# First layer's inputs by quarters of the features

## The chip, the cores and the metric

One core of one Trainium2 chip runs the kernel. The metric is the device time of one execution in microseconds, lower is better. Three runs of the kernel before took 2805.35, 2808.10 and 2808.39 us; the median is 2808.1.

## The reference, cut to what matters

The model is two blocks one after the other over 512 tokens of 1024 features, all float32: a first block of two layers with modulation and several mixers, then a second block with its own mixers and feed-forward layers. The change touches the very beginning, the first layer's normalised and modulated inputs and the first projection made of them. A second stream, ctx, has 256 tokens and runs through the first layer too.

```
m = silu(cvec) @ w_ada + b_ada             # w_ada is 1024 x 3072; cvec is c for x, c_ctx for ctx
sh, sc, gt = split(m, 3)
h  = rms(x,   norm_w) * (1 + sc)   + sh    # 512 x 1024
hc = rms(ctx, norm_w) * (1 + sc_c) + sh_c  # 256 x 1024
p  = h @ w_in                              # k and v columns of two attentions first: 2 x 256 of 2816
```

sh and sc are needed before any product of h: for feature f, sh[f] and sc[f] are columns f and 1024 + f of the modulation.

## The kernel before, in words

A product in full precision is three matmuls: each operand is split into a rounded high part and a low rest, and high x high, high x low and low x high are added in PSUM (`mm3`, L237). The split of a weight or an input takes a cast on ScalarE and a subtraction on VectorE or GpSimd (`wload` L219, `split` L256).

`layer0_norm` (L429) squares and scales the tokens of one stream and transposes them, feature tile by feature tile (eight tiles of 128 features), so that the features lie on the partitions. `ada0` (L451) makes the modulation columns of one half of the features, for both streams: it loads 512 columns of sh and 512 of sc for each of the eight 128-row blocks of `w_ada`, multiplies them by silu(c) and silu(c_ctx), copies the result, transposes it and adds the bias. The four 32-column groups of TensorE's array take the two row blocks of a pair and sh and sc, so two groups are added up at the end.

`proj_kv0` (L499) is the stage of the change. `inputs(i, h)` modulates and splits four feature tiles of stream i; `products(i, h)` adds their products with the 512 k and v columns into six PSUM banks, one for each of four x and two ctx tiles of 128 tokens. One feature tile is 12 matmuls for x and 6 for ctx. `weights(h)` loads and splits the 512 rows of `w_in` that belong to a half. The code runs ada half 0, weights 0, inputs of x, then products of x while ada half 1 is loaded and multiplied between them; then ctx with half 0, weights 1, and both streams with half 1.

Buffers order the rest. Weights and the first half's first four modulation row blocks share the tag `wraw` (two buffers of 8 KB a partition); the other modulation loads have the tag `ada` (four buffers of 4 KB). A load whose buffer is taken waits until its last reader is through. PSUM transposes and the later modulation products share two banks (`tp`).

No engine runs its instructions in the order of the program. A planner in the compiler goes through the program with modelled times and gives each engine, at each moment, the earliest instruction of the program whose inputs and buffers it takes to be ready. The order is then fixed, and each engine runs its list in order, SyncE its DMA issues too.

Of the kernel before, what the change touches and what calls it, by code (L numbers as in the profile page):

```python
# [9 lines left out]
F32 = mybir.dt.float32  # L10
# [4 lines left out]
ALU = mybir.AluOpType  # L15
AX = mybir.AxisListType
PSUM = bass.MemoryType.PSUM
P = 128
# [78 lines left out]
class Kern:  # L97
# [331 lines left out]
    def layer0_norm(self, i, hcp):  # L429

        xt, nt = self.toks[i]
        ss = self.tl(self.sm, [P, nt], F32, "l0ss")
        sq = self.tl(self.hp, [P, 1024], BF16, "hhi")
        for t in range(nt):
            self.S.activation(sq, xt[:, t, :], AF.Square, accum_out=ss[:, t:t + 1])
        r = self.rsq(ss, 1.0 / 1024, EPS, [P, nt], "nrm")
        for t in range(nt):
            self.V.tensor_scalar(xt[:, t, :], xt[:, t, :], r[:, t:t + 1], None, ALU.mult)
        n = nt * P
        xn = [self.tl(*((self.xp, [P, 512], F32, "x"), (hcp, [P, 256], F32, "xc"))[i]) for _ in range(8)]  # L440
        yield xn, n
        for k in range(8):
            ps = self.tl(self.tp, [P, 512], F32, "tp")
            for t in range(nt):
                self.T.transpose(ps[:, t * P:(t + 1) * P], xt[:, t, k * P:(k + 1) * P], self.ident)
            (self.S.copy if k % 2 else self.V.tensor_copy)(xn[k], ps[:, :n])
            if k == 3:
                yield
        yield

    def ada0(self, h, pool):  # L451

        w = self.I["w_ada"][0][:, 0:2048].rearrange("p (a h n) -> p a h n", a=2, h=2)[:, :, h, :]
        bad, nw = self.col("b_ada", 0), self.col("norm_w", 0)
        ad = self.ad[0]

        def load(k):
            raw = self.tl(pool, [P, 2, 512], F32, "ada", bufs=4)
            self.nc.sync.dma_start(raw, w[k * P:(k + 1) * P])
            return raw  # L460

        raws = []
        if h == 0:
            for k in (0, 2):
                raw = self.tl(self.wp, [P, 2, 2, 512], F32, "wraw")
                for r in range(2):
                    self.nc.sync.dma_start(raw[:, r], w[(k + r) * P:(k + r + 1) * P])
                    raws.append(raw[:, r])
        n0 = len(raws)
        raws += [load(k) for k in range(n0, n0 + 4)]  # L470
        yield

        ps = self.mt() if h == 0 else self.tl(self.tp, [P, 512], F32, "tp")
        for k2 in range(4):
            for r in range(2):
                raw = raws.pop(0)
                for a in range(2):
                    g = 2 * r + a
                    self.T.matmul(ps[32 * g:32 * g + 32, :], self.sT[:, 2 * k2 + r, :], raw[:, a, :], start=(k2 == 0), stop=(k2 == 3))
            if n0 == 0 and k2 < 2:  # L480
                raws += [load(k) for k in (2 * k2 + 4, 2 * k2 + 5)]
            if k2 < 3:
                yield
        sb = self.tl(pool, [P, 2, 512], F32, "ada", bufs=4)[:, 0]
        self.V.tensor_copy(sb, ps)
# [3 lines left out]
        ptv = pt.rearrange("p (b r) -> p b r", b=4)  # L489
        for g in range(4):  # L490
            for i in range(2):
                o = 8 * (g % 2) + 4 * h
                dst = ad[:, i, o:o + 4]
                self.V.tensor_tensor(dst, ptv[:, :, 32 * g + i], bad[:, o:o + 4] if g < 2 else dst, ALU.add)
        o = 4 * h
        for i in range(2):
            self.V.scalar_tensor_tensor(ad[:, i, 8 + o:12 + o], ad[:, i, 8 + o:12 + o], 1.0, nw[:, o:o + 4], ALU.add, ALU.mult)

    def proj_kv0(self, ada, st, hcp):  # L499


        ap = self.pool(st, "qkv")
        kvt = [self.tl(ap, [P, 6, 256], F32, "hkv", bufs=2) for _ in range(2)]
        acts, res = [[], []], []
        norms = [self.layer0_norm(i, hcp) for i in range(2)]

        def inputs(i, h):
# [8 lines left out]
        def products(i, h):  # L516
            for k in range(4):
                for tt in ((0, 1, 2, 3), (4, 5))[i]:
                    hi, lo = (t[:, tt % 4 * P:(tt % 4 + 1) * P] for t in acts[i][4 * h + k])
                    self.mm3(pss[tt], hi, lo, w[0][:, k, :], w[1][:, k, :], h + k == 0, h == 1 and k == 3)  # L520
                yield

        def weights(h):
            return self.wload([self.I["w_in"][0][512 * h:512 * h + 512, c0:c0 + 256].rearrange("(k p) n -> p k n", p=P)
                               for c0 in (256, 1024)], 4, 512)

        res.append(next(norms[0]))
        next(norms[0])
        for _ in ada:
            pass  # L530
        w = weights(0)
        self.toks.append(self.load_tok(self.l0p, 1))
        inputs(0, 0)
        pss = [self.mt() for _ in range(6)]
        ada = self.ada0(1, self.l0p)
        next(ada)
        pr = products(0, 0)
        next(pr)
        next(norms[0])
        next(pr)  # L540
        next(ada)
        res.append(next(norms[1]))
        next(norms[1])
        inputs(1, 0)
        next(ada)
        for _ in pr:
            pass
        next(norms[1])
        for _ in ada:
            pass  # L550
        for _ in products(1, 0):
            pass
        w = weights(1)
        inputs(0, 1)
        inputs(1, 1)
        for _ in itertools.chain(products(0, 1), products(1, 1)):
            pass
# [597 lines left out]
    def every(self, gen, n):  # L1155

        for _ in gen:
            for _ in range(n):
                yield
# [1215 lines left out]
```

## Time and profile before

| | us |
|---|---|
| median of three runs | 2808.1 |
| profiled execution | 2807.09 |
| its span (first to last instruction) | 2805.3 |
| TensorE busy in the span | 2712.3 |
| first product of the projection starts | 34.24 |
| its last product ends, about | 80.3 |

The span is what the profiler saw of one execution; durations are read from it. A timeline row gives start, duration, engine, line, operation, output<-inputs, shape and count; in brackets the engine's idle time before it and what ended it. "SPq" is a DMA issue of SyncE, "PE" a matmul of TensorE ("MATMUL" is also a transpose), DVE is VectorE, ACT ScalarE, POOL GpSimd. Rows with a count above 1 cover several instructions in a row.

### The profile page before, as it was taken

Reading aid. Unit: us, or ns where it says so; the run is one execution under the profiler, and the core shown is the slowest. Engines: PE = TensorE matmul, PEld = TensorE weight load, DVE = VectorE, ACT = ScalarE, POOL = GpSimd, SP = SyncE. Lnnn points to the kernel's source line nnn. Section 1 sums busy time; section 2 is a strip of 40 time slices with the busy share of each in tenths; the row PEclk is TensorE's granted clock in tenths of the full one; section 3 lists DMA queues with packets and bytes.
Section 4 is the critical chain, followed back from the end, with each engine's and each line's share of the span. In section 5 each row is a group of like instructions: output and inputs, shape, how many; then the busy total and the mean of one; then the engine's idle time right before and its main releaser. Section 6 shows DMA issues by size and latency. Waiting matters only on the chain. (4 is left out here: it accounts for less than half of the span.)

```text
span 2805.3 us, 39529 instructions
## 1 busy us (share of the span) xinstructions
PE 2712.3 (97%) x15800; PEld 2259.3 (81%) x15800; DVE 1426.3 (51%) x2790; ACT 1001.8 (36%) x1804; POOL 916.7 (33%) x701
## 2 busy tenths in 40 slices
PE   7999999999998999999999989999999989999998
PEld 4976888888897888888988766788888866788888
DVE  5635511113255556434677787655542377655532
ACT  3335522222343553333445342422222344422322
POOL 4500343333234133333322235633333221333332
PEclk9999999999999999999999999999999999999999
DMA  7226222212222114342322230233233212332322
GB/s 248 68 85 201 64 64 69 63 57 68 91 78 90 46 49 122 119 134 76 95 84 71 52 100 31 76 92 104 90 98 98 79 54 84 101 102 91 97 95 87
DMA packets 221580, 250.32 MB, mean 89 GB/s; under 512 B 14351, under 2 KB 205428, under 8 KB 220116
## 3 DMA queue, kind: packets, MB, share of 16 engines
q1 hardware_dynamic: 219204, 242.86, 27.8%
q0 software_dynamic: 2192, 4.93, 0.9%
q8 instruction: 124, 2.03, 0.3%
q14 instruction: 60, 0.49, 0.1%
HBM read 233.64 MB, written 8.88 MB: 86 GB/s over the span
## 5 line engine op out<-in xcount | busy, mean ns | idle before, releaser
L234 POOL TENSOR_TENSOR wlo<-wraw,whi 128x1024 fp32r<-128x1024 f32 (+3 forms) x180 | 437.6, 2431 | 830.6 <-ACT whi L233 809.0
L233 ACT CAST whi<-wraw 128x1024 fp32r<-128x1024 f32 (+2 forms) x360 | 352.1, 1007 | 587.1 <-issue 197.9
L234 DVE TENSOR_TENSOR wlo<-wraw,whi 128x1024 fp32r<-128x1024 f32 (+2 forms) x180 | 235.6, 1309 | 376.0 <-ACT whi L233 375.5
L240 PE MATMUL ex<-hhi,wlo 128*128 128x512 f32 x1044 | 408.5, 391 | 6.8 <-DVE wlo L234 6.8
L238 PE MATMUL ex<-hhi,whi 128*128 128x512 f32 x1044 | 410.6, 393 | 0.6 <-ACT whi L233 0.6
L239 PE MATMUL ex<-hlo,whi 128*128 128x512 f32 x1044 | 408.4, 391 | 0.0
L238 PE MATMUL mm<-hhi,whi 128*128 128x512 f32 x708 | 281.8, 398 | 2.5 <-ACT whi L233 2.5
L239 PE MATMUL mm<-hlo,whi 128*128 128x512 f32 x708 | 279.1, 394 | 3.0 <-DVE hlo L330 2.6
L240 PE MATMUL mm<-hhi,wlo 128*128 128x512 f32 x708 | 279.2, 394 | 2.6 <-DVE wlo L234 2.5
L240 PEld LDWEIGHTS ex<-hhi,wlo 128*128 128x128 f32 x1044 | 196.9, 189 | 49.6 <-DVE wlo L234 8.4
L238 PEld LDWEIGHTS ex<-hhi,whi 128*128 128x128 f32 x1044 | 197.1, 189 | 41.7 <-ACT whi L233 1.2
L239 PEld LDWEIGHTS ex<-hlo,whi 128*128 128x128 f32 x1044 | 197.2, 189 | 39.7 <-issue 0.2
L238 PEld LDWEIGHTS mm<-hhi,whi 128*128 128x128 f32 x708 | 133.8, 189 | 32.8 <-issue 3.8
L240 PEld LDWEIGHTS mm<-hhi,wlo 128*128 128x128 f32 x708 | 133.7, 189 | 32.0 <-DVE wlo L234 3.6
L239 PEld LDWEIGHTS mm<-hlo,whi 128*128 128x128 f32 x708 | 133.7, 189 | 31.3 <-DVE hlo L330 3.9
L238 PE MATMUL mm<-whi,hhi 128*128 128x256 f32 (+1 forms) x464 | 135.5, 292 | 2.1 <-ACT hhi L258 2.1
L240 PE MATMUL mm<-whi,hlo 128*128 128x256 f32 (+1 forms) x464 | 133.3, 288 | 1.4 <-DVE hlo L330 1.4
L239 PE MATMUL mm<-wlo,hhi 128*128 128x256 f32 (+1 forms) x464 | 133.1, 287 | 0.6 <-DVE wlo L234 0.6
L238 PE MATMUL ex<-fhi,whi 128*128 128x512 f32 (+1 forms) x308 | 112.1, 364 | 0.0
L240 PE MATMUL ex<-fhi,wlo 128*128 128x512 f32 (+1 forms) x308 | 111.8, 363 | 0.0
L239 PE MATMUL ex<-flo,whi 128*128 128x512 f32 (+1 forms) x308 | 111.7, 363 | 0.0
L234 POOL TENSOR_TENSOR wblo<-wbraw,wbhi 128x256 fp32r<-128x256 f32 x32 | 27.0, 844 | 238.9 <-ACT wbhi L233 229.0
(827 smaller groups left out, 6024.4 us busy)
## 6 DMA issues: line engine op xcount, KB each, us to landing
wraw<-in_w_merge SPq DMA_DIRECT2D x32, 1024.0 KB
wraw<-in_ev_w_in SPq DMA_DIRECT2D x22, 1024.0 KB
wraw<-in_ffn_gate SPq DMA_DIRECT2D x22, 1024.0 KB
wraw<-in_ffn_up SPq DMA_DIRECT2D x22, 1024.0 KB
wraw<-in_w_in SPq DMA_DIRECT2D x20, 1024.0 KB
wraw<-in_ffn_down SPq DMA_DIRECT2D x17, 1024.0 KB
wraw<-in_w_ada SPq DMA_DIRECT2D x16, 1024.0 KB
wbraw<-in_w_br SPq DMA_DIRECT2D x32, 256.0 KB
```

The costliest lines, as they stand in the source:

```text
L233: self.S.copy(hi[:, a:b], raw[:, a:b])
L234: e.tensor_tensor(lo[:, a:b], raw[:, a:b], hi[:, a:b].bitcast(F32), ALU.subtract)
L238: self.T.matmul(ps, lh, rh, start=first, stop=False)
L239: self.T.matmul(ps, lh, rl, start=False, stop=False)
L240: self.T.matmul(ps, ll, rh, start=False, stop=last)
```

## The change

Quarters take the place of halves. `ada0(q)` makes the columns of 256 features of sh and of sc: eight loads of 128 x (2 x 256), four column groups for four row blocks, four partial sums that a reduction adds. The first quarter's eight row blocks lie in the two `wraw` buffers, the later quarters' in the four `ada` buffers, two row blocks in each. `layer0_norm` yields after every second feature tile. `inputs` and `products` do two feature tiles at a time; the matmuls of the products stay the same, 96 for x and 48 for ctx in all. ctx's first quarter is multiplied after the third quarter of x, its last three after the last of x. The copy of the modulation sums has a buffer of its own.

```diff
-            if k == 3:
+            if k % 2 and k < 7:
                 yield
...
+        w = self.I["w_ada"][0][:, 0:2048].rearrange("p (a h n) -> p a h n", a=2, h=4)[:, :, q, :]
+        for k in range(0, 8, 4 if q == 0 else 2):
+            if q == 0:
+                raw = self.tl(self.wp, [P, 4, 2, 256], F32, "wraw")
+            else:
+                raw = self.tl(pool, [P, 2, 2, 256], F32, "ada", bufs=4)
+            for r in range(raw.shape[1]):
+                self.nc.sync.dma_start(raw[:, r], w[(k + r) * P:(k + r + 1) * P])
+                raws.append(raw[:, r])
+        yield
+        ps = self.mt() if q == 0 else self.tl(self.tp, [P, 512], F32, "tp")
+        for k in range(8):
+            g = k % 4
+            self.T.matmul(ps[32 * g:32 * g + 32, :], self.sT[:, k, :], raws[k].rearrange("p a n -> p (a n)"), start=(k < 4),
+                          stop=(k >= 4))
             if k == 3:
                 yield
...
+        sb = self.tl(pool, [P, 512], F32, "adasb")
+        V.tensor_copy(sb, ps)
         pt = self.tl(self.tp, [P, 512], F32, "tp")
         for b in range(4):
             self.T.transpose(pt[:, b * P:b * P + P], sb[:, b * P:(b + 1) * P], self.ident)
+        ptv = pt.rearrange("p (b g r) -> p b g r", b=4, g=4)
...
+            V.tensor_reduce(t, ptv[:, :, :, i], AX.X, ALU.add)
+            V.tensor_tensor(two(ad[:, i]), t.rearrange("p (a j) -> p a j", a=2), two(self.col("b_ada", 0)), ALU.add)
+            o = ad[:, i, 8 + 2 * q:10 + 2 * q]
+            V.scalar_tensor_tensor(o, o, 1.0, self.col("norm_w", 0)[:, 2 * q:2 * q + 2], ALU.add, ALU.mult)
...
-            for k in range(4 * h, 4 * h + 4):
+            for k in range(2 * q, 2 * q + 2):
...
         res.append(next(norms[0]))
         next(norms[0])
+        every(ada)
+        weights(0)
         inputs(0, 0)
         pss = [self.mt() for _ in range(6)]
+        for q in range(4):
+            ada = iter(())
+            if q < 3:
+                ada = self.ada0(q + 1, self.l0p)
+                next(ada)
+            if q == 0:
+                self.toks.append(self.load_tok(self.l0p, 1))
+            if q == 1:
+                weights(1)
+            pr = products(0, q)
+            next(pr)
+            next(norms[0], None)
+            next(ada, None)
+            every(pr)
+            if q == 1:
+                res.append(next(norms[1]))
+                next(norms[1])
+            every(ada)
+            if q < 3:
+                inputs(0, q + 1)
+            if q == 1:
+                inputs(1, 0)
+            if q == 2:
+                next(norms[1])
+                inputs(1, 1)
+                every(products(1, 0))
+                next(norms[1])
+                inputs(1, 2)
+        every(products(1, 1))
+        every(norms[1])
+        inputs(1, 3)
+        every(products(1, 2))
+        every(products(1, 3))
```

## Rows read from the trace of the kernel before

**Rows 1.** The page, part 1: engine, busy us (share of the span), instructions.
```profile
PE 2712.3 (97%) x15800; PEld 2259.3 (81%) x15800; DVE 1426.3 (51%) x2790; ACT 1001.8 (36%) x1804; POOL 916.7 (33%) x701
```

**Rows 2.** Table by stretches; per engine busy us, then granted clock, DMA share, GB/s.
```profile
0.00:18.00 18.00, 2.25 (x3) 0.37 (x3) 3.49 (x21) 6.09 (x10) 11.33 (x26) 1.00 0.81 277
...
28.60:34.20 5.60, 2.38 (x16) 1.70 (x16) 4.82 (x15) 2.62 (x4) 2.34 (x1) 1.00 0.99 348
...
34.20:41.00 6.80, 6.15 (x15) 4.48 (x16) 5.01 (x9) 4.34 (x8) 3.82 (x2) 0.50 0.69 227
...
34.24:80.32 46.08, 45.47 (x200) 32.14 (x201) 26.02 (x61) 16.88 (x34) 21.01 (x20) 0.93 0.52 164
```

**Rows 3.** Timeline of TensorE: start, duration, line, operation.
```profile
26.62 1.92 PE L479 MATMUL mm<-ada,sT 128*32 128x512 f32 x16
...
34.24 0.80 PE L238 MATMUL mm<-whi,hhi 128*128 128x512 f32 x1 [2.09 <-ACT hhi L258]
...
39.22 0.63 PE L238 MATMUL ex<-whi,hhi 128*128 128x512 f32 x1
...
39.65 0.63 PE L239 MATMUL ex<-wlo,hhi 128*128 128x512 f32 x1
...
41.91 0.39 PE L238 MATMUL ex<-whi,hhi 128*128 128x512 f32 x1
...
42.14 0.39 PE L239 MATMUL ex<-wlo,hhi 128*128 128x512 f32 x1
```

**Rows 4.** Timeline of VectorE, 18 to 35 us.
```profile
18.27 2.74 DVE L438 TENSOR_SCALAR xtok<-xtok,nrm 128x1024 f32<-128x1024 f32 x4
...
28.64 0.69 DVE L485 COPY ada<-mm 128x512 f32<-128x512 f32 x1 [1.65 <-PE mm L479]
...
31.36 1.72 DVE L497 SCALAR_TENSOR_TENSOR ada<-ada,vc 128x4 f32<-128x4 f32 x1
...
33.01 1.44 DVE L512 TENSOR_SCALAR x<-x,ada 128x512 f32<-128x512 f32 x3
```

**Rows 5.** Timeline of ScalarE at 28.6 us.
```profile
28.64 1.99 ACT L233 CAST whi<-wraw 128x1024 fp32r<-128x1024 f32 x2 [1.33 <-DMA wraw<-in_w_in]
```

**Rows 6.** Timeline of SyncE's DMA issues.
```profile
21.67 0.92 SPq L229 DMA_DIRECT2D wraw<-in_w_in  x2
...
22.64 0.98 SPq L426 DMA_DIRECT2D xtok<-in_ctx  x2
...
30.49 1.01 SPq L229 DMA_DIRECT2D wraw<-in_w_in  x2
...
45.14 3.08 SPq L459 DMA_DIRECT2D ada<-in_w_ada  x4
```

**Rows 7.** Timelines of TensorE and ScalarE at the second half's columns.
```profile
56.62 1.06 PE L479 MATMUL tp<-ada,sT 128*32 128x512 f32 x6
...
59.12 0.60 PE L488 MATMUL tp<-cst,ada 128*128 128x128 f32 x4
...
61.63 1.89 ACT L258 CAST hhi<-x 128x512 fp32r<-128x512 f32 x3 [2.42 <-DVE x L512]
...
63.92 0.40 PE L238 MATMUL mm<-whi,hhi 128*128 128x512 f32 x1
```

**Rows 8.** DMA totals of two stretches, 17 to 21 and 55 to 60 us.
```profile
DMA packets 838, 1.39 MB, mean 348 GB/s; under 512 B 154, under 2 KB 170, under 8 KB 838
...
DMA packets 1684, 1.67 MB, mean 334 GB/s; under 512 B 61, under 2 KB 1684, under 8 KB 1684
```

**Rows 9.** Timeline of GpSimd at 83 us.
```profile
83.09 2.41 POOL L234 TENSOR_TENSOR wlo<-wraw,whi 128x1024 fp32r<-128x1024 f32 x1
```

**Rows 10.** Timeline of TensorE, 84 to 86 us.
```profile
84.66 0.63 PE L618 MATMUL tp<-cst,wsp 128*128 128x128 f32 x4 [0.81 <-DMA wsp<-in_w_sp]
...
85.25 0.28 PE L239 MATMUL ex<-wlo,hhi 128*128 128x256 f32 x1
...
85.37 0.28 PE L240 MATMUL ex<-whi,hlo 128*128 128x256 f32 x1
```

More of the change, by code (lines that the diff above doesn't have):

```diff
@@ L446, in layer0_norm, with ada0 @@
             (self.S.copy if k % 2 else self.V.tensor_copy)(xn[k], ps[:, :n])
+            if k % 2 and k < 7:
+                yield
+        yield
+    def ada0(self, q, pool):
+        w = self.I["w_ada"][0][:, 0:2048].rearrange("p (a h n) -> p a h n", a=2, h=4)[:, :, q, :]
+        V, ad = self.V, self.ad[0]
+        raws = []
+        for k in range(0, 8, 4 if q == 0 else 2):
[6 more added lines that the diff above has]
+                raws.append(raw[:, r])
+        yield
+        ps = self.mt() if q == 0 else self.tl(self.tp, [P, 512], F32, "tp")
[3 more added lines that the diff above has]
+                          stop=(k >= 4))
@@ L447, in layer0_norm @@
             if k == 3:
                 yield
[L449 to L485, printed above, removed]
@@ L488, in ada0 @@
             self.T.transpose(pt[:, b * P:b * P + P], sb[:, b * P:(b + 1) * P], self.ident)
[L489 to L495, printed above, removed]
-        for i in range(2):
-            self.V.scalar_tensor_tensor(ad[:, i, 8 + o:12 + o], ad[:, i, 8 + o:12 + o], 1.0, nw[:, o:o + 4], ALU.add, ALU.mult)
+        ptv = pt.rearrange("p (b g r) -> p b g r", b=4, g=4)
+        two = lambda x: x.rearrange("p (a k) -> p a k", k=8)[:, 0:2, 2 * q:2 * q + 2]
+        for i in range(2):
+            t = self.tl(self.sm, [P, 4], F32, "adat")
+            V.tensor_reduce(t, ptv[:, :, :, i], AX.X, ALU.add)
+            V.tensor_tensor(two(ad[:, i]), t.rearrange("p (a j) -> p a j", a=2), two(self.col("b_ada", 0)), ALU.add)
+            o = ad[:, i, 8 + 2 * q:10 + 2 * q]
+            V.scalar_tensor_tensor(o, o, 1.0, self.col("norm_w", 0)[:, 2 * q:2 * q + 2], ALU.add, ALU.mult)
     def proj_kv0(self, ada, st, hcp):
@@ L503, in proj_kv0, with inputs @@
         kvt = [self.tl(ap, [P, 6, 256], F32, "hkv", bufs=2) for _ in range(2)]
-        acts, res = [[], []], []
+        acts, res, ws = [[], []], [], []
         norms = [self.layer0_norm(i, hcp) for i in range(2)]
-        def inputs(i, h):
+        def inputs(i, q):
             xn, n = res[i]
             a, b, _ = self.nb[0][i]
-            for k in range(4 * h, 4 * h + 4):
+            for k in range(2 * q, 2 * q + 2):
                 hi, lo = (self.tl((self.hp, hcp)[i], [P, n], F32R, "hc"[i] + m) for m in ("hi", "lo"))
@@ L514, in inputs, with products @@
                 acts[i].append((hi, lo))
-        def products(i, h):
-            for k in range(4):
+        def products(i, q):
+            for k in range(2 * q, 2 * q + 2):
+                w = ws[k // 4]
                 for tt in ((0, 1, 2, 3), (4, 5))[i]:
-                    hi, lo = (t[:, tt % 4 * P:(tt % 4 + 1) * P] for t in acts[i][4 * h + k])
-                    self.mm3(pss[tt], hi, lo, w[0][:, k, :], w[1][:, k, :], h + k == 0, h == 1 and k == 3)
+                    hi, lo = (t[:, tt % 4 * P:(tt % 4 + 1) * P] for t in acts[i][k])
+                    self.mm3(pss[tt], hi, lo, w[0][:, k % 4, :], w[1][:, k % 4, :], k == 0, k == 7)
@@ L521, in products, with every @@
                 yield
         def weights(h):
-            return self.wload([self.I["w_in"][0][512 * h:512 * h + 512, c0:c0 + 256].rearrange("(k p) n -> p k n", p=P)
-                               for c0 in (256, 1024)], 4, 512)
+            ws.append(self.wload([self.I["w_in"][0][512 * h:512 * h + 512, c0:c0 + 256].rearrange("(k p) n -> p k n", p=P)
+                                  for c0 in (256, 1024)], 4, 512))
+        def every(gen):
+            for _ in gen:
+                pass
         res.append(next(norms[0]))
@@ L528, in proj_kv0 @@
         next(norms[0])
[L529 to L532, printed above, removed]
+        every(ada)
+        weights(0)
         inputs(0, 0)
         pss = [self.mt() for _ in range(6)]
[L535 to L557, printed above, removed]
+        for q in range(4):
[26 more added lines that the diff above has]
+                inputs(1, 2)
```

## The prediction, made before the change was run

> **What bounds the kernel now.** The page comes first: TensorE is busy for 97% of the span [rows 1], so whatever the first stage takes is passed on to the end one for one, as long as TensorE is not left waiting later. The table by stretches comes next [rows 2]. Up to 18 us TensorE does 2.25 us of work; from 28.6 to 34.2 it is busy for only 2.38 of 5.60 us with the DMA engines full (0.99); from 34.24 to 80.32 it runs almost without a pause (45.47 of 46.08 us) and the DMA share is 0.52. So the stage has two parts: a start that waits for data and for a chain of small instructions, and 46 us in which TensorE is the bound. An earlier first product moves the border between them; a pause put into the second part is lost in full.
>
> The timelines show what ends the wait. On TensorE the products for the first half of the modulation columns end at 26.62 + 1.92 = 28.54, and the first product of the projection comes at 34.24, released by a cast of ScalarE [rows 3]. VectorE's timeline shows the chain between: a copy at 28.64, small adds, two scalings, of which one is held from 31.36 to 33.08, then the inputs at 33.01 [rows 4]. The projection's weights landed just as late: ScalarE's cast of them waits for their DMA until 28.64 [rows 5]. SyncE issued them at 21.67 [rows 6].
>
> The order on the engines is not the program's: the second half's weights went out at 30.49, ahead of modulation loads at 45.14 that stand before them in the program [rows 6]. What is ready by the planner's own times goes first; those times I can't see.
>
> **The change part by part.** All times are against the profiled execution (2807.1 us, 1.0 below the median of the runs, 2808.1; its span 2805.3 has 1.8 around it).
>
> *Earlier first product.* The first quarter needs 2.1 MB of modulation weights where the half needed 4.2. Ahead of its last byte lie 0.76 MB of constants and vectors and 2.1 MB of x: 4.96 MB. The engines had moved 277 GB/s x 18.0 = 4.99 MB by 18.0 us [rows 2], so with some 1.5 to land it is there at 19.5. Then x is the later side: its scaling ends at 18.27 + 2.74 = 21.0 [rows 4], and TensorE has its first transposes and the rest of the quarter's products to about 22. The chain from copy to first product took 28.64 to 34.24 = 5.6 us, up to 1.7 of it the held scaling: 3.9 to 5.6, so inputs at 26.0 to 27.7. The weights need the first buffer that the modulation products free. That was at 21.6 before and is about 21 now (the same 1 MB, in four loads for two). Issue 0.9 [rows 6], 1.05 MB at 334 GB/s [rows 8] 3.1, about 1 to land: 26.0; first cast 1.0 [rows 5]: 27.0. Both sides meet at 27.0, that is **7.2 us earlier**. Bounds: 26.0 (the buffer free 1 us sooner; gain 8.2), and 30.3 if the second quarter's 2.1 MB are issued ahead of the weights (6.3 us of DMA, less the 3 us that the queue would else stand still; gain 3.9).
>
> *The boundaries of quarters.* There were two sets of columns; there are four, and each ends in the same chain: copy, four transposes, reduction and small operations, scaling, cast. At the second half of before it ran from the last product at 56.62 + 1.06 = 57.68 to the end of the first cast at 61.63 + 0.63 = 62.26: 4.6 us [rows 7]. There it cost nothing, since ctx products stood on TensorE up to 63.92. A quarter has less to put there. Its 24 products for x take 24 x 0.228 = 5.5 us (from the starts at 41.91 and 42.14 [rows 3]) and stand ahead of the next quarter's last modulation products in the program. After the first quarter nothing else is ready: ctx is loaded behind the second quarter's 2.1 MB, so at 35 at the earliest, and then needs squares, scaling and transposes. So 4.6 us of idle, its four transposes (0.60 [rows 7]) within it. After the second quarter there are eight ctx transposes (about 0.9) and, if the planner pulls them up, 12 ctx products (2.7): 3.7 or 1.0 idle. After the third the program has both there: 1.0, or 0 if a second ctx quarter is pulled up too. In program order that makes 9.3, pulled up 5.6, and 0 if all is filled. I take **+5.6**, since the rows show an order by readiness.
>
> *More transposes.* Sixteen for eight, two groups of four at 0.60. Within a gap they are counted; beside it **+0.6** (bounds 0 and 1.3).
>
> *DMA by smaller pieces.* Modulation weights come in rows of 1 KB where they had 2 KB, and in 32 loads of 256 KB for 16 of 512. A stretch of 1 KB packets moved 334 GB/s, one with mostly 2 KB 348 [rows 8]: 4%, 0.25 us a quarter, hidden behind x in the first and behind products later; bare, 1 us in all. The Trainium skill, DMA: Bandwidth & Descriptors, section Rules for kernel authors, asks for 1 MiB or more per DMA, and its section Bandwidth gives 138 GB/s at 64 KB. By that a quarter could take up to 2.1 MB / 138 = 15 us, an estimate from that page, and the first product would slip past 34; the 348 GB/s were made of 512 KB loads lying one behind another, which speaks against it, though no row has loads of 256 KB. I put it at **0**. SyncE has 16 more issues of at most 0.8 us each (3.08 for four), 12 us if bare; from 31.5 to 45.14 it issues nothing [rows 6], which covers them.
>
> *VectorE.* Two more copies of 0.69 and a few small operations lie in the chains above. The scalings, casts, splits and products keep their number.
>
> *Clock.* The first 12 products ran 0.43 us apart (39.22, 39.65), not 0.23 [rows 3]: 2.4 us. The granted clock was 0.50 from 34.2 to 41.0, its lower level (1.2 GHz), after 2.38 busy of 5.60 us [rows 2]. The start after the change is as thin, so that cost stands: **0** (bounds -2.4, if the transposes keep it at 2.4 GHz, and +2.4 for each gap after which it falls again).
>
> *The end of the stage.* The next weights take the high and low buffers of the first half. They were free at 63.92, 16 us before use; now ctx's second quarter holds them until 24 products (5.5 us) before the end. Casts of 1.0 and 1.0 and GpSimd's 2.41 [rows 5, 9] take 4.4: just covered, **0**, or up to 2 if ctx's splits go first on GpSimd.
>
> Sum: -7.2 + 5.6 + 0.6 = **-1.0 us**, 2806.1; I say 2806.
>
> **The rivals.**
> *Gaps filled (faster).* The planner has each next quarter's columns done before the products run out, or fills each boundary with ctx work: -7.2 + 1.3 = -5.9, 2801; if TensorE is at full rate when it starts, -8.3, 2799. For it: order by readiness, and a DMA share of 0.52 once products run, so data is no limit. Against: the second quarter is queued behind the weights, and the first gap has nothing to fill it. 32%, at 2800.
>
> *Half rate after each gap (slower).* At each boundary TensorE stands still for some us and comes back at 1.2 GHz, so the next quarter's first 12 products cost 2.4 us more. Two falls with gaps in program order: -7.2 + 9.3 + 0.6 + 4.8 = +7.5, 2814.6; three with gaps pulled up: -1.0 + 7.2 = +6.2. From there it decides. For it: the clock was at its lower level after 2.1 us of idle behind a thin stretch. The Trainium skill, TensorE: Matmul & The Clock Gate, section HAM oscillation, tells of a kernel whose short batches between waits each start slow, and asks for batches without waits between; this is that mechanism. Against: an idle of 0.81 us ahead of 84.66 left products 0.12 apart (256 columns) [rows 10]. 20%, at 2814.
>
> *No earlier start.* The planner issues the second quarter ahead of the product weights, so the change does not do what it says: the first product comes at 30.3. The second quarter's columns are then done beside the first products and the first gap goes: -3.9 + 1.0 + 1.3 = -1.6, 2805.5. For it: those loads need no buffer to come free, the weights do. Against: ctx needed none either and was issued behind the weights, at 22.64 [rows 6]. 10%.
>
> **How the numbers follow.** Forecast 38% and the third rival 10% end within 0.2% (5.6 us, about what a measurement of this kernel can tell from no change): same 0.48. Gaps filled gives faster 0.32, half rate slower 0.20. Alone, the forecast lies in 2802 to 2811; with rivals of both signs the range is 2797 (filled, full rate, start at 26.0) to 2817 (two falls, late weights).
>
> **What would show it.** First projection product near 27, its weights cast at about 26; a TensorE gap of 4 us or so ahead of the third feature tile, smaller ones later; granted clock 0.50 once, not thrice; the projection's last product near 79. I am wrong if that product ends before 74.5 or after 86, if the first lies past 31, or if TensorE waits at the stage's end for the next weights.

## The result: 2822.0 us, 0.5% slower, and the profile after

Five runs of the changed kernel took 2818.51 to 2822.49 us (median 2822.0), five of the kernel before beside them 2805.35 to 2808.39 (median 2808.09). The ratio is 1.0051, 95% interval 1.0040 to 1.0063: slower by about 14 us, where 2806 was forecast and 2797 to 2817 given as the range. The profiled execution has a span of 2820.5 us for 2805.3, 15.2 more. TensorE is busy for 7.9 us more and idle for 7.3 more than in [rows 1]:

```profile
PE 2720.2 (96%) x15808; PEld 2261.6 (80%) x15808; DVE 1429.6 (51%) x2796; ACT 1000.8 (35%) x1804; POOL 914.6 (32%) x701
```

The table by stretches, with the columns of [rows 2], for the first stage (first product to the last one's end) and for a stretch behind it:

```profile
30.05:85.34 55.29, 48.54 (x231) 31.84 (x231) 29.27 (x71) 16.91 (x34) 21.00 (x21) 1.00 0.53 166
92.20:95.60 3.40, 3.40 (x18) 3.40 (x18) 0.01 (x1) 0.02 (x1) 0.00 (x0) 0.50 0.87 293
```

The stage starts 4.2 us earlier than before and takes 55.3 us for 46.1 [rows 2]: it ends 5.0 us later. It runs at the full rate of 2.4 GHz throughout (1.00 for 0.93), but 31 more matmuls lie in it, and TensorE idles for 6.75 us where it idled for 0.61. The timeline of TensorE shows where:

```profile
30.05 0.50 PE L238 MATMUL mm<-whi,hhi 128*128 128x512 f32 x1 [1.43 <-ACT hhi L258]
...
32.62 0.50 PE L240 MATMUL mm<-whi,hlo 128*128 128x512 f32 x1 [1.38 <-DVE hlo L259]
...
38.59 1.07 PE L470 MATMUL tp<-ada,sT 128*32 128x512 f32 x8
40.55 0.66 PE L478 MATMUL tp<-cst,adasb 128*128 128x128 f32 x4 [0.89 <-DVE adasb L475]
41.04 1.23 PE L445 MATMUL tp<-cst,xtok 128*128 128x128 f32 x8
42.47 1.07 PE L470 MATMUL tp<-ada,sT 128*32 128x512 f32 x8 [0.20 <-DVE x L446]
43.65 0.50 PE L238 MATMUL mm<-whi,hhi 128*128 128x512 f32 x1
...
55.80 0.63 PE L445 MATMUL tp<-cst,xtok 128*128 128x128 f32 x4 [2.14 <-DVE ada L484]
...
84.30 0.50 PE L240 MATMUL ex<-whi,clo 128*128 128x512 f32 x1 [1.29 <-POOL clo L259]
...
90.97 0.63 PE L620 MATMUL tp<-cst,wsp 128*128 128x128 f32 x4 [2.10 <-DMA wsp<-in_w_sp]
```

Two waits are boundaries between quarters (40.55 and 55.80), two are subtractions (32.62 and 84.30), and the last lies behind the stage: the wait for wsp (weights of the next stage) has grown from 0.81 [rows 10] to 2.10 us, and then the clock falls to its lower level, 1.2 GHz, from 92.2 to 95.6. By 103 us the changed kernel is 7.8 us behind (the start of the same matmul in both). From there on both kernels issue the same instructions in the same order on every engine, and still 7.4 us more are lost by the end.

VectorE's timeline has the reason for three of these waits, GpSimd's stands under it:

```profile
30.03 2.54 DVE L259 TENSOR_TENSOR hlo<-x,hhi 128x512 fp32r<-128x512 f32 x1 [0.23 <-ACT hhi L258]
...
51.82 0.69 DVE L475 COPY adasb<-tp 128x512 f32<-128x512 f32 x1 [0.64 <-PE tp L470]
52.43 3.06 DVE L234 TENSOR_TENSOR wlo<-wraw,whi 128x1024 fp32r<-128x1024 f32 x1
55.41 0.24 DVE L483 TENSOR_REDUCE adat<-tp 128x4 f32<-128x16 f32 x2
```

```profile
29.57 2.45 POOL L234 TENSOR_TENSOR wlo<-wraw,whi 128x1024 fp32r<-128x1024 f32 x1 [12.60 <-ACT whi L233]
...
52.06 2.35 POOL L234 TENSOR_TENSOR wlo<-wraw,whi 128x1024 fp32r<-128x1024 f32 x1 [6.58 <-ACT whi L233]
...
81.17 2.40 POOL L234 TENSOR_TENSOR wlo<-wraw,whi 128x1024 fp32r<-128x1024 f32 x1
83.51 0.73 POOL L259 TENSOR_TENSOR clo<-xc,chi 128x256 fp32r<-128x256 f32 x1
...
86.10 0.76 POOL L613 DMA_DIRECT2D wsp<-in_w_sp  x1 [1.37 <-PE tp L211]
```

VectorE's subtraction of 128x1024 takes 1.23 us when it begins with GpSimd idle (at 28.57) and 3.06 at 52.43; that of 128x512 takes 0.69 (at 43.62, GpSimd idle too) and 2.54 at 30.03. Each long one ends 0.5 to 1.1 us behind the GpSimd subtraction that began before it. The Trainium skill, SBUF — State Buffer, section Who interferes with whom, says that a VectorE instruction with two inputs in SBUF and a GpSimd instruction that reads SBUF lock each other out for a whole instruction, in the order of issue; these four rows agree. At 81.17 GpSimd splits the next stage's weights first, and ctx's last split has to stand behind them.

### The profile page after: what moved, and what is told of

Same layout as the page of the kernel before. It is cut to its first block, busy times and chain, and to the rows that moved or that the text cites. A ratio compares the mean times of both kernels' runs of the same rounds, so it can differ in the third digit from the quotient of the medians.

```text
span 2820.5 us, 39570 instructions
## 1 busy us (share of the span) xinstructions
PE 2720.2 (96%) x15808; PEld 2261.6 (80%) x15808; DVE 1429.6 (51%) x2796; ACT 1000.8 (35%) x1804; POOL 914.6 (32%) x701
```

## The experiments

Three costs had to be told apart: the stage itself (5.0 us), the wait for wsp and the fall behind it (2.7), and the 7.4 us in identical code. For the last there was one lead: the change's new small tag `adat` takes 96 bytes in the pool of small tiles, so 1624 of the later tiles lie 96 bytes higher. Each run stands beside runs of the kernel before on the same chip (medians 2805.9 to 2807.2 us); ratios are to those, with 95% intervals.

**1. The 7.4 us: addresses, time or chance**

The kernel before with the tag alone:

```diff
         self.cst = self.tl(self.cp, [P, CST_KEEP], F32, "cst")
+        self.V.memset(self.tl(self.sm, [P, 4], F32, "adat"), 0.0)
```

> The kernel before, with nothing of the change but its small tag of three [128, 4] buffers in the pool of small tiles, filled once by a memset: from there on 1694 of 2647 tiles stand 96 bytes higher, as 1624 do in the changed kernel. The question: the changed kernel loses 7.8 us by 103 us of the span and 7.4 us more after it, where both kernels issue the same instructions in the same order on every engine. Theory 'addresses': the 7.4 us are the price of the shift by 96 bytes; then this kernel takes 2812 to 2816 us for 2808. Rivals 'time' (the later start moves the clock's falls and the transfers' phase) and 'chance' (the 7.4 us differ from run to run): 2808, within 2.

2810.16 us, ratio 1.0013 (1.0004 to 1.0022): 3.7 us for nothing but the move. Addresses cost, though no more than half of the 7.4.

The changed kernel with the tag in a pool that lies at the other end:

```diff
-            t = self.tl(self.sm, [P, 4], F32, "adat")
+            t = self.tl(pool, [P, 4], F32, "adat", bufs=3)
```

> The changed kernel with the same three small buffers taken from the pool of the first layer's inputs, so that all later tiles stand where they stood before the change. Theory 'addresses': the 7.4 us after 103 us go, and 2814 to 2816 are left of 2822. Rivals 'time' and 'chance': 2820 to 2822.

2815.30 us, 1.0034 (1.0023 to 1.0046). It beats the changed kernel's own ratios (1.0051 above, 1.0045 in part 2) by 0.0017 and 0.0011, 5 and 3 us: the same sum from the other side, though the intervals overlap. In its trace the last 13,800 matmuls take 0.7 us more than in the kernel before; in the changed kernel's trace they take 7.4 more.

The kernel before with a delay at the start:

```diff
+            if gi == 0 and o == 0:
+                for _ in range(50):
+                    self.V.memset(vr, 0.0)
+                self.V.memset(self.cst, 0.0)
```

> The kernel before, with a plain delay of some 7 to 9 us at its start (50 fills of the first loaded tile on VectorE, which the first loads wait for); nothing else is changed, no address either. Theory 'time': a shift of this size alone costs more downstream, 2820 to 2824 in all, with the clock falling at other places. Rivals 'addresses' and 'chance': the delay and no more, 2815 to 2817, and the distance to the kernel before stays level after the delay, within 1 us.

2811.48 us, 1.0020 (1.0010 to 1.0029). The first product came 8.2 us later, the next stage 6.1 later, and the median grew by 5.0: less than the expected 2815, and not more than the delay that was left behind the stage. A later start costs no more than itself, so 'time' as a lasting cost is out; where the clock falls still differs from run to run (see the part on the prediction). Single executions of this kernel ran from 2809.23 to 2816.70, so that one profile can be several us off its median.

The same move by another distance, 128 bytes:

```diff
+        self.V.memset(self.tl(self.sm, [P, 32], F32, "adat", bufs=1), 0.0)
```

> The kernel before with a small tile of 128 bytes more in the pool of small tiles, in place of the 96 bytes of the earlier run, filled once: the same memset, the same 1694 tiles moved, by another distance. Theory 'alignment': a shift by 96 bytes costs through the addresses' remainders, and 128 bytes cost nothing, 2806 to 2808. Rival 'any change': whatever moves the start by part of a microsecond or the tiles by any distance costs the 3.7 us measured for 96 bytes, 2809 to 2811.

2800.63 us, 0.9980 (0.9971 to 0.9989): 5.4 us *faster* than the kernel before. Neither theory had that; but how far the same tiles move changes the sign, so it is a matter of where they come to lie. The trace shows it on the feed-forward's products, which are the same matmuls in all kernels. The view by tile gives duration as min/median/max in ns, for the kernel before, the changed one and the one with 128 bytes:

```profile
L238 PE MATMUL ex<-fhi,whi x308: 279/392/474, 2060.3 to 2794.4; 128*128 128x512 f32 x110, 128*128 128x256 f32 x44
```

```profile
L238 PE MATMUL ex<-fhi,whi x308: 276/395/482, 2075.8 to 2809.5; 128*128 128x512 f32 x110, 128*128 128x256 f32 x44
```

```profile
L239 PE MATMUL ex<-fhi,whi x308: 278/389/476, 2062.6 to 2790.2; 128*128 128x512 f32 x110, 128*128 128x256 f32 x44
```

392, 395 and 389 ns; what counts is the distance from one start to the next, where the same products have medians of 231, 234 and 227. The kernel has 7604 split products of 512 columns. For the some 7140 of them that another one follows at once, at full rate, the distance less 227 ns sums up to:

| kernel | above 227 ns, summed |
|---|---|
| before | 12.1 us |
| changed; before with 96 bytes | 14.4; 14.2 |
| before with 128 bytes | 3.4 |

So 2.3 us of the change's loss are slower products, the same instructions at other addresses, and the kernel before had 8.7 us to win (5.4 measured).

The changed kernel with 32 bytes more, 128 in all:

```diff
+        self.V.memset(self.tl(self.sm, [P, 8], F32, "pad", bufs=1), 0.0)
```

> The changed kernel with a pad of 32 bytes more in the pool of small tiles. In the traces so far, products of 512 columns start 227 ns apart where their moving tile's address leaves the remainder 32 by 256 bytes, and 230 to 234 ns at other remainders; 1924 such products stand at remainder 160 in the kernel before, at 0 in the changed kernel and in the run with 96 bytes, at 32 in the run with 128 bytes. Theory 'remainder': with the pad they stand at 32 and all 9.5 us between the runs with 96 and 128 bytes come back: 2809 to 2812. Rival 'chance of the build': any figure between 2812 and 2822, and the same spacing as before the pad.

2807.22 us, 1.0006 (0.9997 to 1.0015), with 3.4 us above 227 ns like the run with 128 bytes. By the ratios that is 10.9 us less than the changed kernel in part 2 (2819.15 us, 1.0045), where the sums give 11.0 and the theory had 9.5. At equal, good addresses the change costs 1.0006 against 0.9980: 7.3 us, near the 7.8 that the traces show by 103 us.

What the rule is, the products alone show, from nine lines like this one with the start of the slice 8 elements further each time:

```diff
+        for i in range(48): T.matmul(ps[i % 4], ws[i % 2], mv[:, 8:520], start=True, stop=True)
```

> The whole computation is left out and the output filled with zeros: only products of 128 by 128 by 512 in the split type, 48 in a row for each of nine starting addresses of the moving tile (32 bytes apart over 256, the first again at the end), the stationary tile at remainder 32 as in most of the kernel; then the same nine with additions on VectorE and copies on ScalarE beside them. Theory 'remainder': remainder 32 by 256 bytes is some 4 to 7 ns a product faster than the others, both times. Rival 'company': the products alone run at one pace at every address, and differ only beside the other engines or not at all, so that the pace in the kernel comes from where its tiles lie to each other.

Timeline of TensorE, each row 48 products from one address of the moving tile; remainders by 256 of these: 224, 0, 32, 64, 96, 128. The stationary tile (the 128x128 operand that TensorE's weight load takes; the moving tile is the one with the 512 columns) is at 32.

```profile
53.66 11.37 PE L2372 MATMUL ps<-mv,wt 128*128 128x512 f32 x48
64.87 11.36 PE L2373 MATMUL ps<-mv,wt 128*128 128x512 f32 x48
76.06 11.07 PE L2374 MATMUL ps<-mv,wt 128*128 128x512 f32 x48
86.97 11.37 PE L2375 MATMUL ps<-mv,wt 128*128 128x512 f32 x48
98.17 11.16 PE L2376 MATMUL ps<-mv,wt 128*128 128x512 f32 x48
109.17 11.37 PE L2377 MATMUL ps<-mv,wt 128*128 128x512 f32 x48
```

Remainder 32 is the fast one (starts 227.2 ns apart), 96 the second (229.1), all others 233 to 234. VectorE and ScalarE in fact worked beside the first six of the first nine groups, the fast one among them, and beside none of the second nine; both gave the same to 0.5 ns, so 'company' is out. But stationary and moving tile were both at 32:

> The whole computation is left out and the output filled with zeros: products of 512 columns at the nine starting addresses of the moving tile with the stationary tile at remainder 128 by 256 bytes, then the same with 256 columns. Theory 'moving tile': remainder 32 is again the fast one, 227 ns for 512 columns against 233 to 234. Rival 'pair': the fast one moves with the stationary tile, to remainder 128. For 256 columns half the difference, 3 ns, if the loss is by the column; the whole 6 ns if it is by the product.

Stationary tile at 128; moving tile at 128, 160, 192, and further down 32 and again 128:

```profile
20.05 11.04 PE L2369 MATMUL ps<-mv,wt 128*128 128x512 f32 x48
30.93 11.37 PE L2370 MATMUL ps<-mv,wt 128*128 128x512 f32 x48
42.13 11.16 PE L2371 MATMUL ps<-mv,wt 128*128 128x512 f32 x48
...
75.54 11.40 PE L2374 MATMUL ps<-mv,wt 128*128 128x512 f32 x48
...
109.16 11.05 PE L2377 MATMUL ps<-mv,wt 128*128 128x512 f32 x48
```

The rival 'pair' is right, and 'remainder' was a wrong reading of the kernel, where most stationary tiles stand at 32. With the stationary tile at 32 and at 128, what counts is the moving tile's address less the stationary's, by 256: 0 gives 226.7 to 227.2 ns, 64 gives 229.1, the rest 233 to 234. In seven traces of the whole kernel, some 42,000 products at difference 0 have a median of 227, some 500 at 64 of 231, some 3200 at 128 and 4300 at 224 of 232. With 256 columns the spread is 2 ns (117.8 to 119.9), difference 0 among the slower.

The whole kernels also show that this rule is not all. In the changed kernel and in the run with 96 bytes, 329 of these starts lie between products whose tiles both stand at remainder 0, so at difference 0, and they are 231 ns apart in the median; in the kernel before, the same 329 have both tiles at 160 and a median of 227. This alone is 1.3 us of the 2.3. And in the kernel before, 90 products with difference 0 whose successor's stationary tile stands 128 off have a median of 233, so that the pair that counts may be a product's moving tile and the next one's weights. No run tests either.

**2. The changed kernel again, and the end of its stage**

> The changed kernel once more, beside its variants on one chip. The theory of three parts (5.0 us at the end of the first stage, 2.7 us at the wait for wsp and the half rate behind it, some 4 us from the addresses' shift by 96 bytes) gives 11 to 12 us over the kernel before: 2817 to 2819 where that takes 2806.5. If the run after the wsp wait adds a lasting 7.4 us, as in the first trace: 2820 to 2822.

2819.15 us, 1.0045 (1.0031 to 1.0058), at the upper end of the first expectation; the wait for wsp was 1.80 us here and no fall came behind it.

The vectors' transposes moved forward, so that the space that wsp takes over comes free:

```diff
+        self.setup_cols()
         every(products(1, 1))
         every(norms[1])
...
-            self.setup_cols()
             self.setup2_load()
```

> The changed kernel with the transposes of the two other groups of vectors (which the load of wsp waits for, since it takes over their space) moved from the end of the stage to before the last 40 products of the first layer. Theory: the wait of 2.1 us for wsp at 91 us of the span and the half rate at 92.2 to 95.6 us behind it (1.2 us more than at full rate) were of the change's making, through the late release; the load is issued some 1.4 us earlier, at 84.7 for 86.1, 1 to 2.6 us come back, and 2819 to 2821 are left. Rival: the load waits for something else that is as late (GpSimd's own queue), and 2822 stays.

2815.45 us, 1.0033 (1.0020 to 1.0046). GpSimd issues the load at 81.08 for 86.10, and TensorE no longer waits for it, nor does the clock fall behind it:

```profile
87.91 0.60 PE L620 MATMUL tp<-cst,wsp 128*128 128x128 f32 x4
```

The load does hang on these transposes, as the theory had it. What that is worth is not shown: the two ratios differ by 3.4 us, more than the 1 to 2.6 expected, but their intervals overlap, and this run's trace is 6.1 us behind the kernel before at 103 us, where two traces of the changed kernel are 7.8 and 5.4 behind. In it the clock was 0.50 from 54.8 to 61.6 us, and with the load ahead on GpSimd, ctx's last split comes later (TensorE waits 1.77 us for it at 86.87, for 1.29).

**3. GpSimd's part**

```diff
-            for a, b, e in ((0, h, self.V), (h, kt, self.G)):
+            for a, b, e in ((0, h, self.V), (h, kt, eng or self.G)):
...
-                                  for c0 in (256, 1024)], 4, 512))
+                                  for c0 in (256, 1024)], 4, 512, eng=self.V))
...
-                self.split(hi, lo, xn[k], eng=self.G if k % 2 else self.V)
+                self.split(hi, lo, xn[k])
```

> The changed kernel with the subtractions of the first layer's splits (weights and inputs, odd feature tiles too) on VectorE, none on GpSimd. Theory 'hold': VectorE's subtraction of 2.54 us at 30.0 and of 3.06 us at 52.4 (1.23 us alone) and the wait of 1.29 us at 84.3 come from GpSimd's 2.4 us subtractions beside or ahead of them; less VectorE's own added work on the path (0.6 us a quarter), 1 to 3 us come back: 2816 to 2819. Rival: VectorE's order is the bound of each boundary, and 0.6 to 1.2 us more a boundary make it 2820 to 2824.

2816.63 us, 1.0039 (1.0027 to 1.0052); by the intervals alone not apart from the changed kernel's. The trace is clearer: the stage takes 52.6 us for 55.5, TensorE's idle time in it 4.25 for 6.56, and the wait of 1.38 us at the start is gone, since VectorE's split of two tiles now takes 1.29:

```profile
31.72 1.29 DVE L259 TENSOR_TENSOR hlo<-x,hhi 128x512 fp32r<-128x512 f32 x2
```

The wait ahead of ctx's last split stays, at 1.09 us, now for VectorE, and behind the stage the wait for wsp grew to 2.87 us in this trace, with the clock at its lower level from 90.0 to 93.4. Pad, early vectors and no GpSimd together:

> The changed kernel with the pad of 32 bytes, the two groups of vectors transposed before the last 40 products, and the first layer's subtractions on VectorE. Theory: three separate costs (addresses 9.5, late wsp and half rate 1 to 2.7, holds by GpSimd 2.5) add: 2804 to 2808. Rival: the costs share waits, and no more than the pad's gain shows, 2809 to 2812.

2800.84 us, 0.9985 (0.9977 to 0.9994): 5.9 us less than with the pad alone, the sum of the two single gains (3.4 and 1.7 by the ratios) within the intervals. All that the change loses is there again, but no more: the kernel before with the same addresses took 2800.63. In the trace the first product comes at 28.41, 5.8 us ahead of the kernel before, TensorE waits for wsp no longer, the clock does not fall up to 790 us, and at 103 us the two kernels are level: nothing of the earlier start is left there.

**4. The boundaries**

A quarter's column products put between the feature tiles of the quarter before:

```diff
-            if q == 1:
-                weights(1)
             pr = products(0, q)
             next(pr)
             next(norms[0], None)
-            next(ada, None)
+            every(ada)
+            if q < 3:
+                inputs(0, q + 1)
+            if q == 1:
+                weights(1)
             every(pr)
...
-            every(ada)
-            if q < 3:
-                inputs(0, q + 1)
-            if q == 1:
                 inputs(1, 0)
```

> The changed kernel with another order of issue: all eight products for the next quarter's columns, their transposes, the scaling and the split stand between the first and the second feature tile's products of a quarter, not behind both, and the second half's weights are split behind that. Theory 'order': the gaps of 4.0 and 2.1 us come from TensorE's order, in which nothing is left to issue while the columns pass VectorE; 12 products (2.7 us) now cover each, and 3 to 6 us come back: 2813 to 2817. Rival 'transfer': the columns' weights land too late to be used that early, TensorE waits for them in order with the second tile's products behind, and the time stays or grows, 2818 to 2823.

2819.56 us, 1.0049 (1.0036 to 1.0062): nothing, as the rival had it, with a wait of 2.66 us for the cast of the second half's weights at 53.73. The clock fell twice within the stage, which took 57.6 us. With the three corrections besides:

> The run with all three corrections (pad, early vectors, no GpSimd; 2800.8 us) and besides it the other order of issue: a quarter's column products between the feature tiles of the quarter before. Theory 'order': TensorE's waits at the boundaries (0.9, 0.5 and 1.4 us there) and the fillers around them shrink, 2796 to 2799. Rival 'late weights': the second half's weights land at 50 us and TensorE waits for them with all of the second half behind, as in the earlier run of this order (2.7 us there, then the clock fell): 2800 to 2804.

2801.97 us, 0.9980 (0.9971 to 0.9989), the same as without it. Its timelines show what a boundary is. TensorE (last products of the columns, their transposes, the first product of the next quarter) and VectorE between:

```profile
45.22 1.04 PE L471 MATMUL tp<-ada,sT 128*32 128x512 f32 x2
...
47.23 0.60 PE L479 MATMUL tp<-cst,adasb 128*128 128x128 f32 x4
...
51.19 0.80 PE L239 MATMUL mm<-whi,hhi 128*128 128x512 f32 x1 [2.66 <-ACT whi L234]
```

```profile
46.31 0.69 DVE L476 COPY adasb<-tp 128x512 f32<-128x512 f32 x1 [3.93 <-PE tp L471]
47.87 0.25 DVE L484 TENSOR_REDUCE adat<-tp 128x4 f32<-128x16 f32 x2 [0.87 <-PE tp L479]
48.07 0.24 DVE L485 TENSOR_TENSOR ada<-adat,vc 128x4 f32<-128x4 f32 x2
48.27 0.24 DVE L487 SCALAR_TENSOR_TENSOR ada<-ada,vc 128x2 f32<-128x2 f32 x2
48.47 1.00 DVE L502 TENSOR_SCALAR x<-x,ada 128x512 f32<-128x512 f32 x2
49.70 1.29 DVE L260 TENSOR_TENSOR hlo<-x,hhi 128x512 fp32r<-128x512 f32 x2 [0.23 <-ACT hhi L259]
```

From the columns' last product (46.26) to the next quarter's first (51.19) are 4.9 us; one feature tile's 12 products cover 2.7 of such a chain at most. In this run ScalarE's cast of the second half's weights ended it.

An earlier load of those weights (`load1` issues the two DMAs of `weights(1)`, whose split stays where it was):

```diff
             if q == 0:
+                w1 = load1()
                 self.toks.append(self.load_tok(self.l0p, 1))
```

> The same with the load of the second half's weights issued right behind the second quarter's column weights, ahead of the context and of the third quarter's loads, which wait for their buffers until 39 us while the transfers run at 131 to 241 GB/s. Theory 'late weights': the wait for them goes and the order pays, 2794 to 2798. Rival 'order': the weights were not what the boundaries waited for, and the time is that of the run without the earlier load, within 2.

2804.07 us, 0.9988 (0.9979 to 0.9997), no better. The wait for the weights went, but the third quarter's columns came later, TensorE now waited 0.89 and 1.89 us at that boundary for VectorE and ScalarE, and the clock fell twice. That the order pays once the weights are early is refuted.

Two quarters, then a half (`ada0h` makes the second half's columns as the kernel before does; ctx's first half stands behind the second quarter's products):

```diff
...
+        pr = products(0, 0)
+        next(pr)
+        next(norms[0])
+        every(ada)
+        inputs(0, 1)
+        ada = self.ada0h(self.l0p)
+        next(ada)
...
+        every(products(1, 1))
+        weights(1)
+        every(ada)
+        for i in range(2):
+            inputs(i, 2)
+            inputs(i, 3)
```

> The first half's columns in two quarters as in the changed kernel, the second half's as in the kernel before, the pad so that the moved tiles leave the remainder 32; the second quarter's column products stand between the first quarter's feature tiles, and the context's first half is spread behind them. Theory 'boundaries': the changed kernel lost its earlier start of 4 us at the boundaries, not by the start; with one boundary fewer to cross (two for three) and the longest one covered by 24 products of the context, the next stage starts 1 to 5 us earlier than in the kernel before: 2796 to 2800. Rival 'work': TensorE was already full from the first product on in the kernel before, the earlier start only moves work behind it, and the time is that of the padded kernel, 2800 to 2803; if the columns of the second half land late, 2804 to 2808.

2806.02 us, 0.9999 (0.9991 to 1.0008), 5.3 us by the ratios behind the kernel before at the same addresses, against the theory and beyond the first rival. The first product came at 29.28, but the second half's columns landed late (waits of 2.13, 0.66 and 1.46 us from 65 to 68 us, then half rate for 6.8 us): the last rival.

**5. A version that beats both**

The kernel before with 128 bytes of pad and no GpSimd in the first layer's splits, and then its vectors' transposes ahead of the last 24 products:

> The kernel before with 128 bytes of pad and the first layer's subtractions on VectorE. If GpSimd's part costs the kernel before something as well (its TensorE idles 2.1 us ahead of the first product and 0.6 us behind it, then runs at half rate), 1 to 3 us beside the padded kernel's 2800.6: 2798 to 2800. If VectorE is the bound there, 2801 to 2803.

```diff
-        for _ in itertools.chain(products(0, 1), products(1, 1)):
+        for _ in products(0, 1):
+            pass
+        self.setup_cols()
+        for _ in products(1, 1):
             pass
```

> The kernel before with 128 bytes of pad, the subtractions on VectorE (2799.5 us), and the transposes of the two groups of vectors moved ahead of its last 24 products. Theory: its own wait for wsp of 0.8 to 1.1 us goes, and 2798 to 2799 are left; more (2795 to 2797) if the clock's falls move with it. Rival: the transposes take from the products what they give back behind, 2799 to 2800.

2799.53 us, 0.9976 (0.9967 to 0.9984), and 2798.57 us, 0.9968 (0.9955 to 0.9980). By the ratios the pad is 5.6 of these 9.0 us; the two other gains (1.1 and 2.2) are no larger than the intervals are wide. In the second run's trace the first product comes at 32.41 for 34.24, no fall follows it, and the wait for wsp is gone.

## Why the prediction was wrong, step by step

The forecast had the stage end 1.0 us earlier and nothing behind it. The traces have it end 5.0 us later, with 2.7 us more by 103 us and 7.4 behind that. The 6.0 us within the stage are, to 0.1: 3.0 that the first product came later than forecast, 3.6 of moved work, 0.4 of idle time and 0.8 of slower ctx products above the forecast, less 1.7 that the clock gave back.

*Earlier first product: 7.2 us, measured 4.2.* The columns' side held: the inputs' scaling began at 27.09. The weights were cast from 27.48, not 26.0, and ScalarE did more than the one cast of the sum ahead of the first product:

```profile
27.00 0.59 ACT L446 COPY x<-tp 128x512 f32<-128x512 f32 x1 [2.96 <-PE tp L445]
27.48 2.00 ACT L233 CAST whi<-wraw 128x1024 fp32r<-128x1024 f32 x2
29.38 1.14 ACT L258 CAST hhi<-x 128x512 fp32r<-128x512 f32 x2
```

Both halves of the weights and the first input tile, 2.57 us for 1.0. The late cast was not for data: SyncE issued the weights at 19.84, and its own wait for their landing was over at 25.27. ScalarE's list has a copy of x's transposes ahead of the casts, and that copy waited 2.96 us for TensorE; the sum had the cast wait for nothing but the transfer. The bound of 30.3 holds 30.05 by luck: it was for weights issued behind the second quarter, and they went first.

*The step that failed most within the stage is the use of those microseconds.* The sum took the earlier start as gain in full. But TensorE had been full from the first product on [rows 2], and part of what it did ahead of that product now came behind. From the starts of all matmuls between the first product and the vectors' transposes, in us:

| | before | after |
|---|---|---|
| transposes of x and ctx | 2.64 (20) | 4.39 (32) |
| column products | 5.79 | 7.18 |
| transposes of columns | 0.36 (4) | 1.42 (12) |
| products of x | 25.38 | 23.64 |
| products of ctx | 11.32 | 12.12 |
| idle | 0.60 | 6.56 |
| sum | 46.3 | 55.5 |

(Numbers in brackets are counts; the sums include 0.2 for the vectors' transposes, and waits below 0.15 us stand with the matmuls.) Transposes and column products, moved or added, are 4.2 us more, where the prediction had 0.6 for transposes: the whole earlier start.

*The boundaries: 5.6 forecast.* Idle time grew by 6.0 us, near the figure by luck, since it is made of other parts. The boundaries themselves are 0.89, 0.20, 0.49 and 2.14, together 3.7: the first, forecast at 4.6, took 4.0 us from 39.66 to 43.65, most of it filled with transposes and with the next quarter's column products, and the second, forecast at 1.0, was made longer by the held subtraction at 52.43. The other 2.7 us are the waits at 32.62 and 84.30, which the prediction had as 0.

*Clock: 0.* It was -1.7 us: the products of x ran at full rate from the start. The rival of falls after every gap did not happen in this profile; in runs with the other order two came. One fall came behind the stage, after 2.10 us of idle, and cost about 1.2 us by its matmuls' spacing.

*The end of the stage: 0, or up to 2.* 1.29 us, with the order turned round: the next weights went first on GpSimd and ctx's split had to wait. That wsp's load hangs on the transposes of the vectors, and these on the last product, was not followed up, though [rows 10] showed the wait: 1.3 us more for it, 1.2 at half rate.

*DMA by smaller pieces: 0.* No run isolates it, but no wait on the path of the stage is put down to a load of columns, and from 25.3 to 29.8 us, with the second quarter's 256 KB loads one behind another, the engines moved 349 GB/s; the slow loads that the prediction weighed did not come.

*What no step had:* the address of a tile. 2.3 us by the products' spacing, 3.7 measured in the kernel before. Stage, wsp and fall (7.8) and this make 10.1 to 11.5 of 13.9 us. Most of the rest, in these two traces, is the clock behind the stage. Set against each other matmul by matmul, the two traces put 2.1 of the 7.4 us on split products of 512 columns at full rate, 3.9 on matmuls that ran at 1.2 GHz in at least one of the two (51.2 us of the last 13,800 matmuls in the changed kernel, 44.4 in the kernel before), 1.9 on longer waits of TensorE and -0.6 on all others. One fall alone is 3 us. The same matmuls in the changed kernel and in the kernel before, columns as in [rows 2], in both kernels 0.7 to 0.8 us behind the end of an idle time of 1.63 us:

```profile
1788.60:1795.40 6.80, 6.80 (x20) 5.49 (x21) 3.00 (x15) 0.00 (x0) 0.00 (x0) 0.50 0.00 1
```

```profile
1775.90:1779.70 3.80, 3.79 (x20) 3.28 (x21) 2.37 (x13) 0.00 (x0) 0.00 (x0) 1.00 0.01 2
```

That the change makes such falls more frequent is not shown: the time at the lower level was 37.5 to 54.6 us in the six traces with the changed kernel's addresses, 41.0 to 47.8 in the three with those of before, 41.0 to 68.3 in the eight with the good ones. The last 13,800 matmuls took 2498.0 to 2504.2 us in the six, 2495.7 to 2498.8 in the three and 2486.9 to 2496.3 in the eight, and the longest of the eight is the one with 68.3 us.

*The rivals.* None came true as worded. The measured time lies beyond the slower one, by another mechanism: the stage itself ran at full rate, and the falls that cost time lie behind it. "Last product after 86" was missed by 0.5 us and "first past 31" by 1.0, and the third sign, a wait at the stage's end behind the next weights, did show.

## What to carry to other kernels

Where an engine is full behind a start, as TensorE here, an earlier start is worth only the idle time it removes: count which of the engine's own instructions move behind the border before taking the difference as gain, and give each new boundary its whole chain (here 4.9 us) and the work that really stands ready to cover it. A change that allocates anything moves what lies behind it: before a difference of half a per cent is put down to the edit, compare the spacing of identical instructions far from it, and run the edit once more with its tiles padded to the same addresses. Here 32 bytes gave the changed kernel back 11 of the 14 us. And where two traces of the same code differ, set them against each other instruction by instruction and look at the granted clock first.

## What the hardware showed that was not expected

The pace of a split product of 512 columns hangs on how the addresses of its two tiles stand to each other. With the stationary tile at remainder 32 and at 128 by 256 it is 226.7 to 227.2 ns where their difference is a multiple of 256 bytes, 229 at 64 and 233 to 234 elsewhere, alone as well as beside busy engines. The difference is not all: with both tiles at remainder 0, 329 products of the changed kernel have a median of 231. So the count alone does not tell the change's loss. Of the kernel's 7604 such products 1796 stood off difference 0 before, 1508 of them at 128; the change left 1700 off, 1436 at 224, fewer and yet slower in sum, and 128 bytes of pad 360. On the chip 96 bytes cost 3.7 us and 128 bytes gave 5.4.

After the same idle time of 1.63 us, ahead of the same matmuls, the granted clock went to its lower level in one trace and stayed at full rate in another; the one fall cost 3 us.
